# Attention steps at later, written-out places, a raised priority in the recurrent layer, and the low weight parts of the attention on GpSimd

## The chip, the cores and the metric

The kernel runs on one core of one Trainium2 chip. The time is device microseconds (us) of one execution, the median of three runs. The core has a matrix engine (TensorE, PE in the profile; its weight loads are the row PEld), VectorE (DVE), ScalarE (ACT), GpSimd (POOL) and SyncE (SP), which issues the transfers here.

## The reference

512 tokens of width 1024 pass through two layers in float32:

```python
# layer 0
h = h + hybrid_attention_mixer(rms_norm(h))   # 8 dilated heads ("A"), 4 differential heads ("B")
h = h + conv_ffn(rms_norm(h))                 # up 1024 -> 6144, causal conv3, gelu(g) * v, down
# layer 1
h = h + recurrent_mixer(rms_norm(h))          # gate branch * RG-LRU(conv4(x branch))
h = h + conv_ffn(rms_norm(h))
```

The mixer of layer 0 projects to q, k and v, normalises q and k per head, adds a bias that is linear in the distance, takes softmax rows and multiplies by v. A B head subtracts lambda times a second softmax from the first and normalises its output. In the recurrent mixer a block-diagonal product makes the gates r and i of each 128 channels, `a = exp(-8 r softplus(-a_param))`, `u = sqrt(1 - a^2) * (i * x)`, and a scan over time gives h.

## The kernel before

Activations are kept transposed, 128 channels by 512 tokens. Each float32 product is made of three float32r products: an operand is split into a high part (a cast on ACT) and a low part (the difference to it, rounded), and high x high, high x low and low x high are added in PSUM. So each weight tile that comes in is split: `split` (line 97) casts `wh` on ACT (line 100) and subtracts `wl` on DVE (line 102). Weights of the attention's projection come in units of 768 columns, all others in units of 1024. Four buffers each hold the raw, high and low units, and a unit is split two units before TensorE uses it (`AHEAD`).

**The attention.** Eight pairs of heads, first the four B heads (n = 0 to 3), then the eight A heads in pairs (n = 4 to 7), are each projected in a tile: four units by four blocks of 128 tokens, that is 16 steps of six matmuls of 384 columns (`group`, lines 339 to 341, tile `pj`). The 128 steps stand in a list, `line`; behind them come 28 steps of three matmuls of 512 columns, the part of the output projection that needs only finished heads (`early_out`). All other work on TensorE in the attention is placed behind one of these steps by hand, with `place(step, f)`, and TensorE's order is kept as written (`pe`). Step 16 n + 15 ends the projection of tile n; then follow:

- `qk_norm` at once, urgent, on ACT and DVE; `qk_transpose` 8 steps later (`qkt`, line 389).
- The attention proper, whose offsets count from step 16 n + 26. Three batches of scores (`sc`, line 419, tiles `S`), for the query blocks (0, 1), (2) and (3), each followed by its softmax: DVE adds the bias and takes the maximum (line 430), ACT takes the exponential (433); in an A pair ACT scales the row (490), in a B head DVE subtracts the second softmax from the first (535).
- The transposes of the four blocks of probabilities (`tr`, line 440, tile `pt`), each copied out by ACT (`pth`, 443) and DVE (`ptl`, 444); an A pair has two per block.
- The product with v (`out`, lines 453 to 463, tile `O`), two of them in an A pair, and the copies out of PSUM (505 to 510 in A; 546, 548 in B).
- In a B head the norm: a sum over channels on TensorE (`obms`, line 553), two steps on ACT and five on DVE (558 to 562), then the split (564, 565).

The offsets come from `spread`, which lays the pieces and some empty places evenly over 15.5 steps. Scores, transposes, outputs and norms share four PSUM banks. On ACT and DVE the order is a scheduler's: among what is ready it takes what comes first in the program, or has been given high priority, and the order is then fixed.

**The recurrent layer.** For each of eight blocks of channels, `lru_in` multiplies by the input weights, runs the convolution (677, 679, 681) and splits the result (`xrh`, 792; `xrl`, 794); `lru_gates` makes two products of three matmuls (`pr`, `pi`) in two PSUM banks, whose readers are sigmoids on ACT (809, 810). Between the gates of n = 3 and the input of n = 5, `lru_scan` takes the first four blocks through exponential, square, root (820, 822, 828) and the scan on DVE (830). Sigmoids, exponentials and roots are kept in program order on ACT by `after`, as each switch loads a table.

Of the kernel before, what the change touches and what calls it, by code (L numbers as in the profile page):

```python
# [12 lines left out]
F32 = mybir.dt.float32  # L13
F32R = mybir.dt.float32r
AF = mybir.ActivationFunctionType
ALU = mybir.AluOpType
# [7 lines left out]
NB = S // P  # L24
# [6 lines left out]

QK_LAG = 8
AT_LAG = 11
SPAN = 15.5

BATCHES = ((0, 1), (2,), (3,))
GAP = 3
TAIL_A = 3
TAIL_B = 3
TOK = 1  # L40
EARLY = 4
V_BUFS = 3
# [21 lines left out]
def trunk(  # L64
# [16 lines left out]
    V, A, T, G = nc.vector, nc.scalar, nc.tensor, nc.gpsimd  # L81
# [7 lines left out]
    mm = ctx.enter_context(tc.tile_pool(name="mm", bufs=4, space=PSUM))  # L89

    uid = [0]

    def nm(s):
        uid[0] += 1
        return f"{s}{uid[0]}"

    def split(src, n=1024):

        hi = whp.tile([P, n], F32R, tag="wh", name=nm("wh"))
        A.copy(hi, src)  # L100
        lo = wlp.tile([P, n], F32R, tag="wl", name=nm("wl"))
        V.tensor_tensor(lo, src, hi.bitcast(F32), ALU.subtract)  # L102
        return hi, lo

    def load(ap, n=1024, parts=1):
# [6 lines left out]
    def wunit(ap, n=1024):  # L112
        return split(load(ap, n), n)
# [10 lines left out]
    def prefetch(n):  # L124
        while todo and len(ready) < n:
            ready.append(wunit(*todo.pop(0)))

    def next_unit():

        prefetch(AHEAD + 1)  # L130
        return ready.pop(0)
# [71 lines left out]
    with ExitStack() as actx:  # L203
# [113 lines left out]
        def group(n, u, b):  # L317

            t = tiles[n]
            if b == 0:  # L320
                if u == 0:
                    t["banks"] = [mm.tile([P, S], F32, tag="mm", name=nm("pj")) for _ in range(NB)]
                if n == 0:
                    if u == 0:
                        t["units"] = first_tile()
                    t["w"] = t["units"][u]
                    prefetch(min(u, 2))
                else:
                    t["w"] = next_unit()
            if n == 0 and u == 3 and b == TOK:  # L330
                with tc.high_priority():
                    token_stats(x_acc[0])
            wh, wl = t["w"]
            tb = slice(b * P, (b + 1) * P)
            o = t["banks"][b][:, :CW]
            for j in range(2):
                k = 2 * u + j
                cw = slice(j * CW, (j + 1) * CW)
                pe(T.matmul(o, xs[k][0][:, tb], wh[:, cw], start=k == 0, stop=False))  # L339
                pe(T.matmul(o, xs[k][1][:, tb], wh[:, cw], start=False, stop=False))  # L340
                pe(T.matmul(o, xs[k][0][:, tb], wl[:, cw], start=False, stop=k == KC - 1))  # L341
            if u == 3 and (n or b >= TOK):
                with tc.high_priority():
                    for e in range(b + 1) if n == 0 and b == TOK else (b,):
                        evacuate(n, e)
# [126 lines left out]
            oT[p] = (hi, lo)  # L472
            return hi, lo

        def nothing():
            pass

        def attn_a(n):

            p = ORDER[n]  # L480
            st = {}

            def sc(blocks):
                if blocks[0] == 0:
                    st["b"] = [head_bias(2 * p + s) for s in range(2)]
                rows = products(tiles[n]["qk"], blocks)
                for i in blocks:
                    for s in range(2):
                        e, r = softmax_row(rows[s, i], i, st["b"][s])
                        A.activation(e, e, AF.Copy, scale=r)  # L490
                        st["e", s, i] = e

            def tr(s, i):
                if i == 0:
                    st["pt", s] = pt_tiles()
                transposed(st["e", s, i], i, *st["pt", s])

            def out(s):
                ps = bank("O")
                pv(ps, tiles[n]["v"], *st["pt", s], s)  # L500
                if s == 0:
                    st["o"] = smp.tile([P, S], F32, tag="o", name=nm("o"), bufs=1)
                    st["t"] = smp.tile([P, S], F32, tag="t", name=nm("t"), bufs=1)
                lo_half, own = ((ps[HD:], slice(0, HD)), (ps[:HD], slice(HD, P)))[s]
                A.copy(st["t"][own], lo_half)
                V.tensor_tensor(st["o"][own], ps[own], st["t"][own], ALU.add)
                if s == 1:
                    hi, lo = o_tiles(p)
                    A.copy(hi, st["o"])
                    V.tensor_tensor(lo, st["o"], hi.bitcast(F32), ALU.subtract)  # L510

            return spread(
                [partial(sc, b) for b in BATCHES],
                [[partial(tr, s, i) for s in range(2)] for i in range(NB)],
                [partial(out, 0), partial(out, 1)], TAIL_A)

        def attn_b(n):

            p = ORDER[n]
            st = {}  # L520

            def sc(blocks):
                if blocks[0] == 0:
                    st["b"] = head_bias(4 + p)
                rows = products(tiles[n]["qk"], blocks)
                for i in blocks:
                    for c in range(2):
                        st[i, c] = softmax_row(rows[c, i], i, st["b"])
                        if c == 0:
                            e0, r0 = st[i, 0]  # L530
                            A.activation(e0, e0, AF.Copy, scale=r0)
                        else:
                            (e0, _), (e1, r1) = st[i, 0], st[i, 1]
                            V.tensor_tensor(r1, r1, lam, ALU.mult)
                            V.scalar_tensor_tensor(e0, e1, r1, e0, ALU.mult, ALU.add)

            def tr(i):
                if i == 0:
                    st["pt"] = pt_tiles()
                transposed(st[i, 0][0], i, *st["pt"])  # L540

            def out():
                o_ps = bank("O")
                pv(o_ps, tiles[n]["v"], *st["pt"])
                st["o"] = smp.tile([P, S], F32, tag="sq", name=nm("ob"))
                A.copy(st["o"], o_ps)
                st["sq"] = smp.tile([P, S], F32, tag="sm3", name=nm("obsq"))
                A.activation(st["sq"], o_ps, AF.Square)

            def norm():  # L550
                o = st["o"]
                ps = bank("obms")
                pe(T.matmul(ps, ones, st["sq"], start=True, stop=True))
                y = smp.tile([P, S], F32, tag="sm3", name=nm("oby"))
                A.activation(y, ps, AF.Ln, bias=epsb)
                A.activation(y, y, AF.Exp, scale=-0.5)
                t = smp.tile([P, S], F32, tag="sq", name=nm("obt"))
                V.tensor_tensor(t, y, y, ALU.mult)
                V.scalar_tensor_tensor(t, ps, EPS, t, ALU.add, ALU.mult)
                V.tensor_scalar(t, t, -0.5 * (1.0 - LAM_INIT), 1.5 * (1.0 - LAM_INIT), ALU.mult, ALU.add)  # L560
                V.tensor_tensor(y, y, t, ALU.mult)
                V.scalar_tensor_tensor(o, o, col(C_BS), y, ALU.mult, ALU.mult)
                hi, lo = o_tiles(p)
                A.copy(hi, o)
                V.tensor_tensor(lo, o, hi.bitcast(F32), ALU.subtract)

            return spread(
                [partial(sc, b) for b in BATCHES], [[partial(tr, i)] for i in range(NB)],
                [out] + [nothing] * TAIL_B + [norm], TAIL_B)

        def spread(scs, trs, outs, tail):

            gap = [nothing] * GAP
            s = [scs[0]] + gap + [scs[1]] + gap + [scs[2]]
            for i, tr in enumerate(trs):
                s += tr + [nothing] * (GAP if i + 1 < NB else tail)
            return s + outs


        early = []  # L580
# [24 lines left out]
        def place(g, f):  # L605
            at.setdefault(int(g), []).append(f)
# [12 lines left out]
        for n in range(NT):  # L619
            place(16 * n + 15, partial(urgent, qk_norm, n))  # L620
            place(16 * n + 15 + QK_LAG, partial(qk_transpose, n))
            steps = (attn_a if ORDER[n] < 4 else attn_b)(n)
            for k, f in enumerate(steps):
                place(16 * n + 15 + AT_LAG + k * SPAN / len(steps), f)
        for g in range(max(len(line), max(at) + 1)):
            if g < len(line):
                line[g]()
# [212 lines left out]

    prev = None
    for n in range(KC):
        cur = lru_in(n)
        if prev is not None:
            lru_gates(n - 1, *prev)
        if n == KC // 2:
            lru_scan(range(KC // 2))
        prev = cur
# [92 lines left out]
```

## Time and profile before

| | |
|---|---|
| median of 3 runs | 1210.08 us (1209.28 to 1210.39) |
| the profiled execution | 1209.16 us, span of its instructions 1207.4 us |
| mean granted TensorE clock | 0.997 of full speed |
| TensorE busy | 1186.1 us (98%), 5566 matmuls |
| DVE, ACT busy | 810.3 us (67%), 581.9 us (48%) |
| GpSimd busy | 0.7 us |

The attention lasts until about 245 us of the span, the recurrent layer's gates lie between 680 and 735 us, and the rest are projections and feed-forward layers. A matmul's end is modelled in the profile, so a wait is shown a little shorter than the distance between two starts. The granted clock is the share of full speed (2.4 GHz) that the chip allowed TensorE; 0.5 is its lower level.

### The profile page before, as it was taken

To read this page: it belongs to the slowest core of one execution; us is meant where nothing else is said; L and a number is where in the kernel's file an instruction comes from. 1 tells how busy PE (TensorE), PEld (TensorE's weight loads), DVE (VectorE), ACT (ScalarE), POOL (GpSimd) and SP (SyncE) were. 2 spreads that over 40 slices of the span, in tenths; PEclk is the share of its full clock that TensorE was granted. 3 is DMA by queue.
4 is the path that set the end of the run, shared out by engine and by line. 5 is a ranking of instruction groups with operands and counts; after the bars stand their busy time and mean duration, and the time that the engine had idled before them with its cause. 6 is when DMAs were issued, how large, how long until landed. Compare 5 with 4: busy or idle time off the path is not lost.

```text
span 1207.4 us, 14660 instructions
## 1 busy us (share of the span) xinstructions
PE 1186.1 (98%) x5566; PEld 989.9 (82%) x5566; DVE 810.3 (67%) x1333; ACT 581.9 (48%) x972; POOL 0.7 (0%) x6
## 2 busy tenths in 40 slices
PE   8999999999999999999999999999999999999998
PEld 8988888778888888888888778888888888888887
DVE  7878877677777773577446887767777763577431
ACT  7666787655444441344224688545444432344220
POOL 0000000000000000000000000000000000000000
PEclk9999999999999999999999999999999999999999
DMA  7221122053323233232323312433233332323221
GB/s 252 79 67 53 53 70 80 19 174 105 105 88 105 89 103 96 97 103 90 104 88 105 117 41 74 136 93 100 91 102 95 98 100 93 105 88 105 88 87 53
DMA packets 33766, 114.31 MB, mean 95 GB/s; under 512 B 3872, under 2 KB 4384, under 8 KB 33696
## 3 DMA queue, kind: packets, MB, share of 16 engines
q1 hardware_dynamic: 33552, 113.37, 29.6%
q8 instruction: 44, 0.72, 0.2%
q14 instruction: 26, 0.21, 0.1%
q10 hardware_dynamic: 144, 0.00, 0.0%
HBM read 111.27 MB, written 2.10 MB: 94 GB/s over the span
## 4 chain that ended last, share of the span: by engine, by line
PE 87%; ACT 7%; DVE 5%; DMA 1%; issue 1%; SPq 0%; ACTq 0%; DVEq 0%
PE mm L116 26%; PE mm L118 26%; PE mm L117 26%; ACT sm L433 2%; PE pj L339 1%; PE pj L341 1%; PE pj L340 1%; PE pt L440 1%; ACT sm L490 1%; DMA raw<-in_w_att_dram 1%; PE qkt L389 1%; ACT wh L100 1%; ACT qkraw L359 1%; DVE wl L102 1%; ACT v L362 0%
## 5 line engine op out<-in xcount | busy, mean ns | idle before, releaser
L116 PE MATMUL mm<-xh,wh 128*128 128x512 f32 x896 | 350.2, 391 | 0.0
L117 PE MATMUL mm<-xl,wh 128*128 128x512 f32 x896 | 349.1, 390 | 0.0
L118 PE MATMUL mm<-xh,wl 128*128 128x512 f32 x896 | 349.0, 390 | 0.0
L100 ACT CAST wh<-raw 128x1024 fp32r<-128x1024 f32 (+1 forms) x207 | 211.4, 1024 | 274.8 <-PE mm L117 245.0
L102 DVE TENSOR_TENSOR wl<-raw,wh 128x1024 fp32r<-128x1024 f32 (+1 forms) x207 | 244.8, 1183 | 42.9 <-ACT wh L100 39.6
L117 PEld LDWEIGHTS mm<-xl,wh 128*128 128x128 f32 x896 | 168.4, 188 | 35.7 <-issue 0.7
L116 PEld LDWEIGHTS mm<-xh,wh 128*128 128x128 f32 x896 | 168.4, 188 | 35.6 <-issue 0.7
L118 PEld LDWEIGHTS mm<-xh,wl 128*128 128x128 f32 x896 | 168.3, 188 | 35.2
L681 DVE SCALAR_TENSOR_TENSOR cv<-us,pt,cv 128x511 f32<-128x511 f32 (+2 forms) x216 | 160.9, 747 | 4.8 <-ACT cv L679 1.2
L116 PE MATMUL mm<-fh,wh 128*128 128x512 f32 x384 | 149.4, 389 | 0.0
L117 PE MATMUL mm<-fl,wh 128*128 128x512 f32 x384 | 149.4, 389 | 0.0
L118 PE MATMUL mm<-fh,wl 128*128 128x512 f32 x384 | 149.4, 389 | 0.0
L677 DVE TENSOR_TENSOR us<-mm,rs 128x512 f32<-128x512 f32 x104 | 71.5, 688 | 94.5 <-PE mm L118 94.4
L711 DVE TENSOR_TENSOR h<-mm,h 128x512 f32<-128x512 f32 x48 | 33.2, 691 | 141.5 <-PE mm L118 141.5
L339 PE MATMUL pj<-wh,xh 128*128 128x384 f32 x256 | 93.4, 365 | 1.6 <-ACT wh L309 0.5
L702 ACT CAST fh<-cv 128x512 fp32r<-128x512 f32 x48 | 29.8, 621 | 126.4 <-DVE cv L699 126.4
L679 ACT ACTIVATE cv<-us,pt 128x512 f32<-128x512 f32 x104 | 84.6, 813 | 11.4 <-DVE us L677 11.2
L341 PE MATMUL pj<-wl,xh 128*128 128x384 f32 x256 | 86.7, 339 | 1.0 <-DVE wl L102 1.0
L340 PE MATMUL pj<-wh,xl 128*128 128x384 f32 x256 | 86.1, 336 | 0.0
L116 PEld LDWEIGHTS mm<-fh,wh 128*128 128x128 f32 x384 | 72.1, 188 | 15.0
L118 PEld LDWEIGHTS mm<-fh,wl 128*128 128x128 f32 x384 | 72.1, 188 | 15.0
L117 PEld LDWEIGHTS mm<-fl,wh 128*128 128x128 f32 x384 | 72.1, 188 | 15.0
(190 smaller groups left out, 1233.3 us busy)
## 6 DMA issues: line engine op xcount, KB each, us to landing
raw<-in_w_up_dram SPq DMA_DIRECT2D x96, 512.0 KB, 3.5
raw<-in_w_dn_dram SPq DMA_DIRECT2D x48, 512.0 KB, 3.5
raw<-in_w_att_dram SPq DMA_DIRECT2D x31, 384.0 KB, 3.1
raw<-in_w_ri_dram SPq DMA_DIRECT2D x16, 512.0 KB, 3.5
raw<-in_w_ao_dram SPq DMA_DIRECT2D x8, 512.0 KB, 3.8
raw<-in_w_ro_dram SPq DMA_DIRECT2D x8, 512.0 KB, 3.5
raw<-in_xT_dram SPq DMA_DIRECT2D x7, 512.0 KB, 4.6
out_dram<-h SPq DMA_DIRECT2D x8, 256.0 KB, 2.0
```

Of the source, the lines that this page charges most:

```text
L100: A.copy(hi, src)
L102: V.tensor_tensor(lo, src, hi.bitcast(F32), ALU.subtract)
L116: order(T.matmul(out, wh, xh, start=first, stop=False))
L117: order(T.matmul(out, wh, xl, start=False, stop=False))
L118: return order(T.matmul(out, wl, xh, start=False, stop=last))
L339: pe(T.matmul(o, xs[k][0][:, tb], wh[:, cw], start=k == 0, stop=False))
L340: pe(T.matmul(o, xs[k][1][:, tb], wh[:, cw], start=False, stop=False))
L341: pe(T.matmul(o, xs[k][0][:, tb], wl[:, cw], start=False, stop=k == KC - 1))
L677: V.tensor_tensor(u, ps, state["rs"], ALU.mult)
L679: A.activation(c, u, AF.Identity, scale=col(wcol + (taps - 1) * stride), bias=col(bcol))
L681: V.scalar_tensor_tensor(c[:, d:], u[:, : S - d], col(wcol + (taps - 1 - d) * stride), c[:, d:], ALU.mult, ALU.add)
L711: V.tensor_tensor(h[m], ps, h[m], ALU.add)
```

## The change

- The offsets are written out. Scores stay at 0, 2, 4 in all tiles. Transposes of a B tile go from steps 4, 6, 8, 10 to 6, 8, 10, 13, its output product from 12 to 15, its norm from 14 to 17, which is behind the first scores of the next tile (16). An A pair's transposes go from 4 and 5, 7 and 7, 9 and 10, 12 and 12 to 6 and 7, 8 and 9, 10 and 11, 13 and 14, its two output products from 14 and 15 to 15 and 16. `qk_transpose` of the next tile stays at 13.
- `split` subtracts the low part on GpSimd instead of DVE for units of 768 columns, once the first step of the line is under way (`warmed`): the units of the first pair stay on DVE.
- `lru_in` and `lru_gates` of the recurrent layer, except the last gates, get high priority.

```diff
-SPAN = 15.5
...
-GAP = 3
-TAIL_A = 3
-TAIL_B = 3
+
+SC_AT = (0, 2, 4)
+TR_AT = (6.5, 8.7, 10.9, 13.1)
+OUT_AT = 15
+NORM_AT = 17
...
+    warmed = []
...
-        V.tensor_tensor(lo, src, hi.bitcast(F32), ALU.subtract)
+        (G if n == 768 and warmed else V).tensor_tensor(lo, src, hi.bitcast(F32), ALU.subtract)
...
                     t["w"] = t["units"][u]
+                    warmed.append(u)
                     prefetch(min(u, 2))
...
-            return spread(
-                [partial(sc, b) for b in BATCHES],
-                [[partial(tr, s, i) for s in range(2)] for i in range(NB)],
-                [partial(out, 0), partial(out, 1)], TAIL_A)
+            steps = [(g, partial(sc, b)) for g, b in zip(SC_AT, BATCHES)]
+            steps += [(g + s, partial(tr, s, i)) for i, g in enumerate(TR_AT) for s in range(2)]
+            return steps + [(OUT_AT + s, partial(out, s)) for s in range(2)]
...
-            return spread(
-                [partial(sc, b) for b in BATCHES], [[partial(tr, i)] for i in range(NB)],
-                [out] + [nothing] * TAIL_B + [norm], TAIL_B)
-
-        def spread(scs, trs, outs, tail):
-
-            gap = [nothing] * GAP
-            s = [scs[0]] + gap + [scs[1]] + gap + [scs[2]]
-            for i, tr in enumerate(trs):
-                s += tr + [nothing] * (GAP if i + 1 < NB else tail)
-            return s + outs
+            steps = [(g, partial(sc, b)) for g, b in zip(SC_AT, BATCHES)]
+            steps += [(g, partial(tr, i)) for i, g in enumerate(TR_AT)]
+            return steps + [(OUT_AT, out), (NORM_AT, norm)]
...
-            for k, f in enumerate(steps):
-                place(16 * n + 15 + AT_LAG + k * SPAN / len(steps), f)
+            for g, f in steps:
+                place(16 * n + 15 + AT_LAG + g, f)
...
-        cur = lru_in(n)
-        if prev is not None:
-            lru_gates(n - 1, *prev)
+        with tc.high_priority():
+            cur = lru_in(n)
+            if prev is not None:
+                lru_gates(n - 1, *prev)
```

## Rows read from the trace of the kernel before

**Rows 1.** The page, busy time of TensorE: us, share, instructions.

```profile
PE 1186.1 (98%) x5566; PEld 989.9 (82%) x5566; DVE 810.3 (67%) x1333; ACT 581.9 (48%) x972; POOL 0.7 (0%) x6
```

**Rows 2.** Waits of TensorE: us in total, times, longest.

```profile
PE pt L440 <- DVE sm L535: 5.2, 6, 1.4
PE pt L440 <- DVE ptl L444: 3.1, 2, 1.8
PE pt L440 <- DVE rst L168: 2.9, 1, 2.9
PE pr L116 <- ACT xrh L792: 2.0, 1, 2.0
...
PE mm L116 <- ACT oh L509: 0.6, 1, 0.6
```

**Rows 3.** Busy us of each engine, then granted clock, in windows of the attention.

```profile
core 0: us, PE busy (x) PEld busy (x) DVE busy (x) ACT busy (x) POOL busy (x), PEclk, DMA share, GB/s
...
90.00:120.00 30.00, 28.20 (x178) 24.96 (x177) 24.34 (x69) 18.59 (x52) 0.00 (x0) 1.00 0.20 59
...
180.00:210.00 30.00, 28.17 (x179) 25.29 (x179) 23.58 (x68) 23.25 (x66) 0.00 (x0) 1.00 0.27 88
```

**Rows 4.** Timeline of TensorE in a B tile: start, us, instruction, [idle before].

```profile
87.90 1.02 PE L553 MATMUL obms<-obsq,ones 128*128 128x512 f32 x2
...
102.45 0.34 PE L341 MATMUL pj<-wl,xh 128*128 128x384 f32 x1
104.21 0.55 PE L440 MATMUL pt<-ident,sm 128*128 128x128 f32 x3 [1.43 <-DVE sm L535]
104.52 0.42 PE L339 MATMUL pj<-wh,xh 128*128 128x384 f32 x1
...
106.53 0.34 PE L341 MATMUL pj<-wl,xh 128*128 128x384 f32 x1
```

**Rows 5.** Windows around the wait of n = 6, columns as in rows 3.

```profile
210.00:213.00 3.00, 1.19 (x6) 0.62 (x4) 2.27 (x7) 3.00 (x8) 0.00 (x0) 1.00 0.01 5
213.00:216.00 3.00, 1.92 (x8) 1.56 (x9) 2.55 (x10) 3.00 (x10) 0.00 (x0) 0.73 0.01 3
216.00:219.00 3.00, 3.00 (x15) 2.54 (x14) 2.65 (x5) 0.74 (x2) 0.00 (x0) 0.70 0.02 5
```

**Rows 6.** Timeline of TensorE in the recurrent layer.

```profile
716.29 0.39 PE L116 MATMUL mm<-xh,wh 128*128 128x512 f32 x1
716.52 0.39 PE L117 MATMUL mm<-xl,wh 128*128 128x512 f32 x1
718.93 0.50 PE L116 MATMUL pr<-xrh,gwh 128*128 128x512 f32 x1 [2.02 <-ACT xrh L792]
```

**Rows 7.** Windows behind that wait, columns as in rows 3.

```profile
719.00:721.00 2.00, 2.00 (x6) 1.62 (x7) 1.98 (x3) 1.54 (x2) 0.00 (x0) 0.64 0.17 14
721.00:723.00 2.00, 2.00 (x6) 1.51 (x6) 2.00 (x4) 0.00 (x0) 0.00 (x0) 0.50 0.66 246
```

**Rows 8.** Timeline of DVE in the B tile of rows 4.

```profile
91.07 0.69 DVE L559 SCALAR_TENSOR_TENSOR obt<-obms,obt 128x512 f32<-128x512 f32 x1
...
101.22 0.96 DVE L102 TENSOR_TENSOR wl<-raw,wh 128x768 fp32r<-128x768 f32 x1
...
103.55 0.61 DVE L535 SCALAR_TENSOR_TENSOR sm<-sm,sum,sm 128x384 f32<-128x384 f32 x1
```

**Rows 9.** Waits of all engines: ACT's for the norm of a B tile.

```profile
ACT oh L564 <- DVE ob L562: 13.8, 4, 3.5
```

**Rows 10.** Groups of DVE by line and form: busy us, mean ns.

```profile
L102 DVE TENSOR_TENSOR wl<-raw,wh 128x768 fp32r<-128x768 f32 x31 | 29.6, 953 | 13.2 <-ACT wh L100 13.0
```

**Rows 11.** Groups of GpSimd, columns as in rows 10.

```profile
masks.py:199 POOL TENSOR_SCALAR_AFFINE_SELECT ident<-ident 128x128 f32<-128x128 f32 x1 | 0.3, 294 | 0.1
```

**Rows 12.** Timeline of ACT in the recurrent layer.

```profile
710.31 0.80 ACT L679 ACTIVATE cv<-us,pt 128x512 f32<-128x512 f32 x1
...
713.01 0.68 ACT L810 ACTIVATE u<-pi,pt 128x512 f32<-128x512 f32 x1
...
718.25 0.62 ACT L792 CAST xrh<-cv 128x512 fp32r<-128x512 f32 x1 [2.07 <-DVE cv L681]
```

More of the change, by code (lines that the diff above doesn't have):

```diff
@@ L473, in o_tiles @@
             return hi, lo
-        def nothing():
-            pass
         def attn_a(n):
```

## The prediction

> **What bounds the kernel now.** I read the page's first part, the waits of TensorE, windows of 30 us, and then timelines around each wait. TensorE is busy for 1186.1 of 1207.4 us [rows 1]; the change can only be worth what TensorE loses, and I looked for where that is. Its waits stand in one short list, and the feed-forward layers are not in it. What matters of it [rows 2]: transposes of the probabilities (`pt`, line 440) wait 5.2 us in 6 places for DVE's `sm` at line 535 (the B tiles), 3.1 us in 2 places for `ptl` and 2.9 us in one place at line 168 (the A tiles); one gate product of the recurrent layer (`pr`) waits 2.0 us, and the output projection 0.6 us. In windows of the attention TensorE runs for about 28 of 30 us, DVE for 24, ACT for 19 to 23 [rows 3]: no engine is full, so it is the order that makes TensorE wait.
>
> What a wait really costs is more than the idle time printed, since ends of matmuls are modelled. In a B tile TensorE's instructions follow each other every 0.18 us (11 steps from 104.52 to 106.53), and the wait at 104.21 follows its predecessor by 1.76 us: 1.6 us lost for 1.43 printed [rows 4]. With 0.16 us added at each of nine places, the `pt` waits cost 6.1 us (B), 3.4 us (tiles n = 4 and 5) and 3.1 us (n = 6), together 12.6. After the last one the granted clock is 0.73 and 0.70 in two stretches of 3 us [rows 5], that is, TensorE at its lower level (1.2 GHz) for some 3.4 us, which costs 1.7 us more; it had idled 2.89 us. After the 1.8 us of n = 5 [rows 2] the window has the full clock, 1.00 [rows 3]. The gate product is alike: 718.93 - 716.52 - 0.23 = 2.2 us lost [rows 6], then 0.64 and 0.50 of the clock over 4 us [rows 7], 1.7 us more: 3.9 us in all. Everything that can be won is so 12.6 + 1.7 + 3.9 + 0.6 = 18.8 us.
>
> **Part by part. Transposes later in B tiles.** A step of the line (six matmuls) lasts 6 x 0.18 = 1.1 us. A B tile's transposes move from offsets 4, 6, 8, 10 to 6, 8, 10, 13, so the two that wait get 2.2 and 3.3 us of other projection matmuls as cover, against 1.6 and 0.6 us lost. At the same time TensorE loses less, so ACT and DVE must do a tile in some 2 us less. DVE can: before the waited `sm` it does a `wl` of 0.96 us at 101.22 [rows 8], which goes away. And the norm, whose five DVE operations ACT waits out for up to 3.5 us per B tile [rows 9], moves behind the next tile's first scores, whose softmax then starts without it. The 6.1 us go. Against that: the norm's sum of squares now holds one of four PSUM banks while three batches of scores want two each. It is held from 87.90 to the end of line 559 at 91.76, 3.9 us [rows 4, 8]; from offset 17 to the third batch at 20 there are three steps, 3.3 us. That is between 0 (another bank is free) and 0.6 us for each of four tiles behind a B tile; I take half, 1.2 us. Net gain 4.9, bounds 3.7 and 6.1.
>
> **Transposes later in A tiles.** Here most of the third block's transposes move by one step (9 to 10, 10 to 11). What they wait for is a PSUM bank, held until the first transposes are copied out, and that copy stands on ACT behind all the exponentials: ACT is busy for all of 210 to 213 us while TensorE has 1.19 of 3 us [rows 5]. ACT keeps all its work, so the offload to GpSimd does not shorten this; one step does: 1.1 us each for n = 4 and 5, 2.2 of 3.4 us. For n = 6 the line has already turned to output products of three matmuls, 3 x 0.23 = 0.7 us a step [rows 6], so 0.7 of 3.1 us goes; the 2.2 us left (2.89 - 0.7) are still above the 2.02 after which the clock fell, so I leave the 1.7 us in. Lower bound nothing, upper bound all (8.2 us with the clock).
>
> **The end of the attention.** The last tile's second output product moves from step 153 to 154 of 155. One step less lies over the chain of copy, add, round that the first output projection waits for (0.6 us now): 0.7 us more.
>
> **Low parts on GpSimd.** Of the 31 `wl` instructions of 768 columns, 28 leave DVE (three stay with the first pair), 28 x 0.953 = 26.7 us [rows 10]. The trace has no two-input arithmetic on GpSimd. Its nearest row is a 128x128 select of 0.294 us [rows 11], six times the width gives 1.8 us as an upper estimate; the lower bound is DVE's 0.95. The latency doesn't show: units are split two ahead, eight steps of 1.1 us before TensorE needs them, and GpSimd has only four such operations per tile, 7 us of 25. Nothing else is queued on GpSimd behind them. The raw buffers come free up to 0.9 us later; there are four, and no wait of TensorE in the attention's steady part comes from a transfer [rows 2]. So on TensorE's path this part costs 0; its gain is inside the B figure. If that cover were gone, each late unit would cost TensorE 1.8 - 0.95 us, 24 us in all.
>
> What could speak against it is that the two engines disturb each other. The trace of before cannot show it, as GpSimd does nothing beside DVE in it but set-up [rows 11]. The Trainium skill, in "SBUF — State Buffer", Who interferes with whom, says that a DVE instruction with two SBUF inputs and a GpSimd instruction that reads SBUF exclude each other for their whole length, whichever starts second waiting. No run yet shows it; by that rule `sm` at line 535 and the norm's products can be held up, and the price is that of the last rival below. The Trainium skill, "GPSIMD Engine Reference", 3.1 Elementwise, gives 4497 ns of a two-input add for 2048 columns, so an estimate of 1.7 us for 768; the sum would be the same.
>
> **Priority in the recurrent layer.** `xrh` of n = 5 comes at 718.25 because its convolution's ACT step (line 679) stands behind the whole first scan, at 710.31, and the rest of the chain takes 8 us more among the scan's DVE steps [rows 12]. Raised ahead of the scan, both go earlier. But the same product also needs the two PSUM banks that the gates of n = 4 free, and these stay behind the scan by an explicit order: the second is read until 713.01 + 0.68 = 713.7 [rows 12]. Work put ahead of the scan (the step of 0.80 us, the rounding of 0.62 us, a weight cast or so) moves that to some 716. That is 3 us before the product ran (718.93), and next to where TensorE came to it (716.52) [rows 6]. So the wait goes if the order on TensorE stays about as it is: 3.9 us. Bounds: all 3.9, or, if the product is put a job earlier (some 29 matmuls of 0.23 us before 716.5, around 710), a wait of 5.8 us plus the clock's 1.7, which is 3.6 us worse than now.
>
> **The sum.** 4.9 + 2.2 + 0.7 - 0.7 + 3.9 = 11.0 us. The profiled execution took 1209.16 us with a span of 1207.4; 1209.2 - 11.0 = 1198.2. The median of the runs is 0.9 above the profiled one, so 1199.
>
> **Rivals.**
> *The A waits go too.* ACT begins the softmax of n = 4 only behind the norm's rounding [rows 9], and between A tiles behind the output chain; if it now begins earlier, the 1.2 + 2.4 + 1.7 us left also go: 1199.1 - 5.3 = 1193.8. Against it: ACT is full in that stretch [rows 5].
> *The gate product waits for its banks instead of for its input.* Place as above, the price between no gain (1203) and 3.6 us worse (1206.6). For it: the banks come free by my reckoning within half a microsecond of when TensorE arrives.
> *New waits in the attention eat its gain* (banks for the scores, the output product behind later transposes): about 7 us lost again, 1206.
> *Slower: GpSimd holds DVE up.* If each of its four operations per tile stopped DVE for its whole 1.8 us, DVE would lose 7.0 and gain 3.8 us, 3.2 more per tile on six tiles, 19.2 us: 1199.1 + 19.2 = 1218. It turns the result from 11.0 / 6 = 1.8 us a tile on. Against it: the operands of most DVE steps on that path (scores, transposes, projections) lie in PSUM, and there is now room. The rule of the Trainium skill named above is this rival.
> That the offload does not happen can be left out: the condition is met for every unit of 768 columns after the first step.
>
> **How the numbers follow.** Chances: forecast 0.47, A waits too 0.18, gate banks 0.18, new waits 0.10, GpSimd slows DVE 0.05, other 0.02. A measurement here tells 0.2% (2.4 us) from no change. Forecast and first rival are faster for sure, the gate rival nearly so; new waits may come out within 0.2%; with the last, slower: faster 0.85, same 0.08, slower 0.07. The range goes from everything gone but the tail (1192.5) to the gate banks at their worst (1207).
>
> **What would show it.** B tiles: no wait of `pt` for line 535, each tile some 2 us shorter. A tiles: waits of some 0.5 to 1 us left at line 440, one above 2 us near n = 6 with a clock below 1. Recurrent layer: no `pr` wait, clock 1.00. GpSimd: 28 operations of 1 to 2 us and about 27 us less on DVE. Wrong would be a wait of `S` for banks, `pr` waiting for line 810, or line 535 lasting longer than its 0.61 us for 384 columns.

## The result, and the profile after

The change makes the kernel slower: 1256.0 us (median of 4 runs, 1253.5 to 1259.3) against 1209.7 on the same chip, a ratio of 1.038 with a 95% interval of 1.036 to 1.041. The forecast was 1199. The profiled execution has a span of 1252.5 us, 45.1 more than before, in two places: the last wait of the attention (`mm` for `oh`) stands at 262.73 us instead of 245.96, 16.8 later, and the other 28.3 us are lost in the recurrent layer.

The page after, busy time, answers to [rows 1]: TensorE idles for 31.5 us more and is busy 13.6 us longer with the same 5566 matmuls (part of them at the lower clock), and DVE is no less busy than before although 28 instructions have left it.

```profile
PE 1199.7 (96%) x5566; PEld 999.1 (80%) x5566; DVE 814.8 (65%) x1305; ACT 582.8 (47%) x972; POOL 54.9 (4%) x34
```

The waits of TensorE after (us in total, times, longest) answer to [rows 2]. Line numbers have moved: `pt` 440 is 444, `pr` 116 is 119, `sm` 535 is still 535, `wh` 100 is 103.

```profile
PE mm L119 <- ACT wh L103: 13.1, 2, 12.1
PE qkt L393 <- DVE qkraw L384: 11.4, 7, 3.9
PE mm L119 <- DVE us L669: 7.3, 1, 7.3
PE pj L343 <- DVE v L367: 5.1, 4, 1.6
PE pt L444 <- DVE ptl L448: 2.8, 2, 2.1
PE S L423 <- DVE ql L398: 2.7, 2, 2.4
PE mm L121 <- DVE wl L105: 1.7, 1, 1.7
```

What the forecast wanted gone is gone: no `pt` waits for line 535, none for 168, and no `pr` waits for `xrh` (two of 0.9 and 0.2 us for others are left). In their place stand waits for other DVE instructions of the attention (`qkraw`, `v`, `ql`) and three of the recurrent layer that were not there at all. No wait of TensorE names GpSimd: its low parts are never late.

What is late is seen in the groups (busy us, mean ns), first the new one on GpSimd, then some of DVE up to 262 us of the span.

```profile
L105 POOL TENSOR_TENSOR wl<-raw,wh 128x768 fp32r<-128x768 f32 x28 | 54.2, 1938 | 154.5 <-ACT wh L103 120.1 <-DVE bias L408 19.9 <-PE pj L345 14.5
```

```profile
L384 DVE TENSOR_TENSOR qkraw<-qkraw,rsy 128x512 f32<-128x512 f32 x16 | 16.8, 1093 | 0.2
L534 DVE TENSOR_TENSOR sum<-sum,lam 128x1 f32<-128x1 f32 x16 | 7.4, 465 | 0.3
L171 DVE TENSOR_TENSOR rst<-rst,ms 128x16 f32<-128x16 f32 x8 | 4.5, 560 | 0.1
L408 DVE TENSOR_SCALAR bias<-dist_b 128x512 f32<-128x512 f32 x4 | 3.1, 786 | 0.0
```

The same groups before:

```profile
L380 DVE TENSOR_TENSOR qkraw<-qkraw,rsy 128x512 f32<-128x512 f32 x16 | 10.3, 683 | 0.1
L534 DVE TENSOR_TENSOR sum<-sum,lam 128x1 f32<-128x1 f32 x16 | 2.5, 155 | 0.2
L168 DVE TENSOR_TENSOR rst<-rst,ms 128x16 f32<-128x16 f32 x8 | 1.3, 168 | 0.1
L404 DVE TENSOR_SCALAR bias<-dist_b 128x512 f32<-128x512 f32 x4 | 1.7, 419 | 0.0
```

A mean hides how this happens; the timeline after of one B tile shows it, first GpSimd, then DVE:

```profile
76.22 1.84 POOL L105 TENSOR_TENSOR wl<-raw,wh 128x768 fp32r<-128x768 f32 x1 [10.30 <-ACT wh L103]
79.95 2.29 POOL L105 TENSOR_TENSOR wl<-raw,wh 128x768 fp32r<-128x768 f32 x1 [1.90 <-ACT wh L103]
86.08 1.84 POOL L105 TENSOR_TENSOR wl<-raw,wh 128x768 fp32r<-128x768 f32 x1 [3.83 <-ACT wh L103]
```

```profile
77.04 0.68 DVE L559 SCALAR_TENSOR_TENSOR obt<-obms,obt 128x512 f32<-128x512 f32 x1
...
80.46 1.80 DVE L534 TENSOR_TENSOR sum<-sum,lam 128x1 f32<-128x1 f32 x1
...
86.33 1.88 DVE L408 TENSOR_SCALAR bias<-dist_b 128x512 f32<-128x512 f32 x1
```

The product of one column per partition at 80.46, 0.16 us of work, ends at 82.26, just when GpSimd's instruction does (82.24); everything behind it in DVE's order is 1.6 us late. The bias at 86.33 is held as well: 1.88 us instead of 0.42, until 0.29 us behind the end of GpSimd's instruction (87.92). GpSimd's instruction from 79.95 is itself 0.45 us longer than the other two; when it started, `ob` of line 562, with its inputs in SBUF, was under way (79.79 to 80.53). Line 559 at 77.04, one of whose inputs lies in PSUM (`obms`), runs beside GpSimd in 0.68 us, as it did before without it (0.69, [rows 8]). The clock pays too: over the first two stretches of 100 us the granted clock is 0.98 and 0.95, before it was 1.00 in both.

In the recurrent layer the timeline after, TensorE, ACT and DVE together, shows both large waits:

```profile
702.75 3.89 ACT L103 CAST wh<-raw 128x1024 fp32r<-128x1024 f32 x4 [4.25 <-PE mm L120]
...
704.14 1.02 PE L652 MATMUL nrm<-acc,ones 128*128 128x512 f32 x2
...
706.54 0.68 ACT L654 ACTIVATE rs<-nrm,epsb 128x512 f32<-128x512 f32 x1
...
711.61 1.89 DVE L669 TENSOR_TENSOR us<-mm,rs 128x512 f32<-128x512 f32 x3
...
712.45 0.77 PE L119 MATMUL mm<-xh,wh 128*128 128x512 f32 x1 [7.29 <-DVE us L669]
...
773.27 1.28 ACT L812 ACT_TABLE_LOAD   x1
...
782.98 2.93 ACT L103 CAST wh<-raw 128x1024 fp32r<-128x1024 f32 x3
784.06 0.80 PE L119 MATMUL mm<-xh,wh 128*128 128x512 f32 x1 [12.13 <-ACT wh L103]
```

Before, TensorE had the norm and the first gate product here:

```profile
669.13 1.02 PE L660 MATMUL nrm<-acc,ones 128*128 128x512 f32 x2
...
681.04 0.50 PE L116 MATMUL pr<-xrh,gwh 128*128 128x512 f32 x1
```

After, the norm `nrm` is computed only behind the projections of four blocks, 96 matmuls, where before it stood behind the first block's 24; the four casts raised with them stand ahead of the norm's first step on ACT, so `us`, which frees the projections' banks, comes at 711.61. Later all projections have been used up ahead of the gates, and nothing is left to run under the second scan (ACT from 773.27): TensorE waits until the scan's last root is through and the first cast behind it is made. Before, 48 matmuls of projections ran between `nrm` and the first gate product, while ACT and DVE made the norm. The granted clock pays here as well (window 760 to 780 us 0.87, 780 to 800 us 0.61).

### The profile page after: what moved, and what is told of

Same layout as the page of the kernel before. It is cut to its first block, busy times and chain, and to the rows that moved or that the text cites. A ratio compares the mean times of both kernels' runs of the same rounds, so it can differ in the third digit from the quotient of the medians.

```text
span 1252.5 us, 14696 instructions
## 1 busy us (share of the span) xinstructions
PE 1199.7 (96%) x5566; PEld 999.1 (80%) x5566; DVE 814.8 (65%) x1305; ACT 582.8 (47%) x972; POOL 54.9 (4%) x34
## 4 chain that ended last, share of the span: by engine, by line
PE 83%; DVE 9%; ACT 5%; issue 2%; DMA 1%; SPq 0%; DVEq 0%; ACTq 0%
PE mm L119 25%; PE mm L121 25%; PE mm L120 25%; PE pj L343 2%; PE pj L345 2%; PE pj L344 2%; DVE qkraw L384 1%; PE S L423 1%; ACT sm L437 1%; PE pt L444 1%; DVE u L822 1%; ACT wh L103 1%; PE qkt L393 1%; DMA raw<-in_xT_dram 1%; DVE wl L105 1%
## 5 line engine op out<-in xcount | busy, mean ns | idle before, releaser
L121 PE MATMUL mm<-xh,wl 128*128 128x512 f32 x896 | 344.5, 392 | 1.9 <-DVE wl L105 1.7
L120 PE MATMUL mm<-xl,wh 128*128 128x512 f32 x896 | 345.0, 392 | 0.0
L105 DVE TENSOR_TENSOR wl<-raw,wh 128x1024 fp32r<-128x1024 f32 (+1 forms) x179 | 218.1, 1222 | 31.7 <-ACT wh L103 28.7
L343 PE MATMUL pj<-wh,xh 128*128 128x384 f32 x256 | 96.1, 376 | 5.7 <-DVE v L367 5.1
```

What stands on the lines that cost most here:

```text
L105: (G if n == 768 and warmed else V).tensor_tensor(lo, src, hi.bitcast(F32), ALU.subtract)
L120: order(T.matmul(out, wh, xl, start=False, stop=False))
L121: return order(T.matmul(out, wl, xh, start=False, stop=last))
```

## The experiments

**The parts alone.** Three kernels each make one part of the change, a fourth all but the priority. The places alone are the change's hunks on `SPAN`, `spread`, `attn_a` and `attn_b`; the others:

```diff
 # GpSimd alone (and the lines of `warmed`)
 ...
-        V.tensor_tensor(lo, src, hi.bitcast(F32), ALU.subtract)
+        (G if n == 768 and warmed else V).tensor_tensor(lo, src, hi.bitcast(F32), ALU.subtract)
 ...
 # priority alone
 ...
+        with tc.high_priority():
             cur = lru_in(n)
             if prev is not None:
                 lru_gates(n - 1, *prev)
```

> The kernel before with the later places alone; all low parts on DVE, no priority in the recurrent layer. Theory 1 (the attention's 16.8 us of loss come from GpSimd shutting DVE out, and the later places are good): the pt waits of 11.2 us go at least by half, time 1200 to 1205 us. Theory 2 (the later places are the loss, through new waits of the key transposes and the score banks): attention about 17 us longer, time 1222 to 1228 us.

> The kernel before with the 28 low parts on GpSimd alone, at the old places. Theory 1: GpSimd holds DVE up by 1.1 us per operation (31 us in all, as in the changed kernel) and the old places have less cover, time 1225 to 1240 us. Theory 2: DVE gets 26.7 us of room and the pt waits shrink, time 1203 to 1210 us.

> The kernel before with the high priority of the recurrent layer's input and gates alone. Theory 1 (the priority pulls the projections ahead of the norm and the gates, so that nothing is left to cover the second scan): 28 us more, time 1234 to 1242 us, with waits of about 7 us before the convolution of the first block and 12 us before a gate projection. Rival (the loss needs the attention's change too, or comes from its clock): time 1205 to 1212 us.

> The changed kernel without the priority of the recurrent layer. If the two stages add up: before plus 16.8 us, 1225 to 1229 us, on either theory of the attention; the recurrent layer again has its single 2.0 us wait. If the stages do not add up, outside of 1222 to 1232 us.

| kernel | us | ratio to before (95%) | difference |
|---|---|---|---|
| before, same chip | 1210.2 | | |
| places alone | 1206.5 | 0.9970 (0.9959 to 0.9981) | -3.7 |
| GpSimd alone | 1235.0 | 1.0210 (1.0193 to 1.0227) | +24.8 |
| priority alone | 1237.0 | 1.0222 (1.0207 to 1.0238) | +26.8 |
| places and GpSimd | 1229.3 | 1.0169 (1.0141 to 1.0198) | +19.1 |

The parts add up: -3.7 + 24.8 + 26.8 = 47.9 against 46.4 for the whole change. The places gain, and each of the other two loses far more.

The waits of the places alone show the gain and what ate half of it:

```profile
PE qkt L393 <- DVE qkraw L384: 4.9, 4, 1.5
PE pt L444 <- DVE ptl L448: 2.1, 1, 2.1
PE pr L119 <- ACT xrh L784: 2.0, 1, 2.0
PE mm L119 <- ACT oh L510: 1.3, 1, 1.3
```

One of the four waits for `qkraw`, in the timeline of TensorE:

```profile
110.24 1.23 PE L393 MATMUL qkt<-ident,qkraw 128*128 128x128 f32 x8 [1.47 <-DVE qkraw L384]
```

With GpSimd alone the stretched groups are others than in the whole change, above all the one that the forecast had named as the sign (0.61 us before, [rows 8], and still 0.61 in the whole change, where no stop met it); TensorE waits for what follows it, now at the output product:

```profile
L537 DVE SCALAR_TENSOR_TENSOR sm<-sm,sum,sm 128x384 f32<-128x384 f32 x4 | 7.2, 1801 | 0.0
L171 DVE TENSOR_TENSOR rsy<-rsy,rst 128x16 f32<-128x16 f32 x8 | 6.0, 749 | 0.2
```

```profile
PE O L457 <- DVE ptl L446: 12.0, 4, 3.3
```

The page of this kernel shows that the 24.8 us are not waiting alone:

```profile
PE 1196.6 (97%) x5566; PEld 998.0 (81%) x5566; DVE 814.9 (66%) x1305; ACT 582.3 (47%) x972; POOL 53.6 (4%) x34
```

Of its span of 1231.3 us (23.9 more than before) TensorE idles for 34.7, which is 13.4 more, and it is busy 10.5 us longer with the same matmuls: the granted clock is 0.95 in both of the first two stretches of 100 us (1.00 before).

**Is it GpSimd's reading?** In three kernels DVE keeps every low part, and GpSimd does something that nobody waits for, at the same places in the program.

```diff
+        if n == 768 and warmed:
+            d = dmp.tile([P, 256], F32, ...)
+            for c in (slice(0, 256), slice(256, 512), slice(512, 768)):
+                G.tensor_tensor(d, src[:, c], hi[:, c].bitcast(F32), ALU.subtract)   # reads two
+                G.tensor_copy(d, hi[:, c].bitcast(F32))        # or: reads one
+            G.tensor_copy(d[:, :1], hi[:, :1].bitcast(F32))    # or: one column, and
+            for _ in range(6):
+                G.memset(d, 0.0)                               # writes only
```

> The kernel before, in which DVE still makes all low parts; GpSimd additionally makes the same 28 differences (three of 256 columns each, some 1.9 us per unit) into an unused scratch buffer. Nothing on another engine needs what GpSimd writes. Theory (GpSimd's reading of SBUF stops DVE's instructions with two SBUF inputs): the same DVE forms are stretched as in the run with the low parts on GpSimd (the difference over 384 columns from 0.61 us to over 1.2, the 128x16 products from 0.17 to over 0.4), and the time is at least as bad as that run's, 25 to 50 us above before, as DVE has kept its 26.7 us. Rival (the harm is that the low parts come later, from a slower engine): nothing is late here, so within 3 us of before and no form on DVE stretched.

> As the run in which GpSimd repeats the differences, but GpSimd only writes: one column copied from the high part (so that it starts at the same place), then six memsets of 256 columns into the scratch buffer. DVE keeps its work. Theory (two inputs from SBUF on GpSimd are what excludes DVE): DVE's forms keep their durations within 10% and the time stays within 4 us of before. Rival (any work of GpSimd, or its writes and semaphores, disturbs DVE): forms stretched in proportion to GpSimd's busy time, 10 us or more above before.

> As the run in which GpSimd repeats the differences into a scratch buffer, but each of the 84 is a copy of 256 columns of the high part: one input from SBUF instead of two. Nothing waits for them. Theory A (any read of SBUF by GpSimd excludes DVE's two-input forms): the same DVE forms are stretched, in proportion to GpSimd's busy time; with some 0.5 us a copy about half the loss of that run, 6 to 14 us above before. Theory B (only two-input instructions of GpSimd exclude DVE): the forms keep their durations within 10%, within 4 us of before.

| GpSimd beside an unchanged DVE | GpSimd busy us | us (before) | ratio (95%) | DVE busy us (810.3 before) |
|---|---|---|---|---|
| 84 differences, two inputs | 86.1 | 1226.6 (1208.5) | 1.0148 (1.0132 to 1.0163) | 830.4 |
| 84 copies, one input | 56.9 | 1212.5 (1210.1) | 1.0024 (1.0012 to 1.0036) | 815.7 |
| memsets, almost only writes | 70.6 | 1210.0 (1208.5) | 1.0012 (1.0003 to 1.0021) | 810.9 |

Groups of DVE with the differences, then with the copies, then with the memsets: two products with both inputs in SBUF, and a scaling with one.

```profile
L173 DVE TENSOR_TENSOR rst<-rsy 128x16 f32<-128x16 f32 x8 | 4.0, 500 | 0.7 <-ACT rsy L171 0.7
L174 DVE TENSOR_TENSOR rst<-rst,ms 128x16 f32<-128x16 f32 x8 | 3.2, 398 | 0.1
L380 DVE TENSOR_SCALAR ms<-ms 128x16 f32<-128x16 f32 x8 | 2.9, 368 | 0.1
```

```profile
L173 DVE TENSOR_TENSOR rst<-rsy 128x16 f32<-128x16 f32 x8 | 2.3, 293 | 0.7 <-ACT rsy L171 0.7
L174 DVE TENSOR_TENSOR rst<-rst,ms 128x16 f32<-128x16 f32 x8 | 1.9, 241 | 0.1
```

```profile
L174 DVE TENSOR_TENSOR rst<-rsy 128x16 f32<-128x16 f32 x8 | 1.4, 170 | 0.7 <-ACT rsy L172 0.7
L175 DVE TENSOR_TENSOR rst<-rst,ms 128x16 f32<-128x16 f32 x8 | 1.4, 170 | 0.1
...
L381 DVE TENSOR_SCALAR ms<-ms 128x16 f32<-128x16 f32 x8 | 2.1, 257 | 0.1
```

The first run settles that it is no lateness: nothing needs what GpSimd makes, and 18 us are lost. GpSimd's reading does hold the raw buffers, and 26 transfers wait for it, by 2.9 us at most; but between 25 and 245 us no cast waits for a transfer and no matmul for a weight part, so that is not the loss. The 18 us are less than the 25 to 50 expected; in three short pieces each stop is shorter, and the 384-column difference happened to meet none of them (608 ns), so that part of the expectation failed. Writes leave the two-input products alone (0.17 us, as before). Copies fall between the theories: the same products are stretched, but by at most some 0.2 us each, and 2.4 us are lost, not 6 to 14.

**Which raised instructions hurt?**

```diff
 # chain raised                             # jobs raised
         ps = job(xs)                       +        with tc.high_priority():
+        with tc.high_priority():           +            ps = job(xs)
+            xr = conv(...); xh, xl = ...           xr = conv(...); xh, xl = ...
 ...
+            with tc.high_priority():
+                lru_gates(n - 1, *prev)            lru_gates(n - 1, *prev)
```

> The kernel before, in which only the convolution, its split and the gates of the recurrent layer get high priority, and the projections (job) keep theirs. Theory (the loss of the recurrent change comes from projections pulled ahead of the norm and of the scan's cover): the order of the projections stays, the 7.3 us wait for us and the 12.1 us wait for wh don't appear, the 2.0 us wait of the first gate product goes with its clock loss of 1.7 us: 1206 to 1208, that is 2 to 4 us faster. Rival (raising the chain delays the scans or casts themselves): the wait for wh behind the second scan stays and the time is 10 us or more above before.

> The kernel before, in which only the projections (job) of the recurrent layer's input get high priority, not the convolution and the gates. Theory (pulled projections are the loss): both new waits are there again, 7 us for us and some 12 us for wh behind the second scan, 20 to 27 us above before. Rival (the raised chain is the loss): within 4 us of before.

The chain alone: 1207.4 against 1208.5, ratio 0.9988 (0.9979 to 0.9997), and 2.6 us less in the span of the profiled executions. The wait of the first gate product shrinks from 2.0 to two of 0.6 and 0.2, and the window from 720 to 740 us has the full clock (0.93 before). The projections alone: 1228.5, ratio 1.0168 (1.0155 to 1.0182), +20.0, with these waits new:

```profile
PE mm L116 <- DVE us L677: 8.6, 2, 7.3
...
PE mm L116 <- ACT wh L100: 4.6, 2, 3.6
```

So the projections are the cause of 20.0 of the 26.8 us. The expected 12 us behind the second scan did not come. The wait of 3.6 us for a cast stands behind the first scan, and through the second (ACT from 763.40) TensorE has no wait:

```profile
750.79 0.80 PE L116 MATMUL mm<-xh,wh 128*128 128x512 f32 x1 [3.60 <-ACT wh L100]
```

Only with the chain raised as well does the cast of the gate input's weights fall behind the whole second scan, with its wait of 12.1 us. With both raised 6.8 us more are lost than with the projections alone; that this cast is the reason is read from the traces, no run shows it apart. The chain alone does no harm.

**What the runs point to.** The places and the raised chain, with nothing on GpSimd; then `QK_LAG` 9 instead of 8, which puts `qk_transpose` one step later, at 14 in the tile; then `AT_LAG` 12 on top.

```diff
-QK_LAG = 8
-AT_LAG = 11
+QK_LAG = 9        # second and third
+AT_LAG = 12       # third
```

> The later places, and high priority for the recurrent chain (convolution, split, gates) without the projections; nothing on GpSimd. Theory (the two act in different layers and add): 3.7 from the places and 1.2 to 2.6 from the chain, so 4.9 to 6.3 us below before; the 4.9 us waits of qkt for qkraw stay. Rival (they share a cause): not below the run with the places alone, 3.7.

> As the run with later places and raised chain, with qk_transpose one step (1.1 us) later, at 14 instead of 13 in its tile. Theory (the scaling of qkraw ends when it did in the kernel before, and TensorE comes to qkt too early because the output product no longer stands ahead of it): of four waits of 1.2 to 1.5 us at most 0.4 us each stay, so 3 to 4.5 us faster than that run, 8 to 10 below before. Rival (DVE takes the slack, qkraw simply comes later, or the scores now wait for ql): the waits stay in sum, within 1.5 us of that run.

> As the run before in this list, with the whole attention of each tile one step later as well (scores at 27 instead of 26), so that the scores keep their distance from qk_transpose. Theory (the one step of qk_transpose was enough and S does not wait): 0.5 to 1.5 us slower than it, as the last tile ends a step later and the output projection waits for oh that much longer (1.3 to some 2.4 us). Rival (S waited for ql in it): that wait goes, and this is the faster by 1 us or more.

Against 1208.7 before on the same chip: 1203.2, ratio 0.9959 (0.9945 to 0.9974); 1199.3, ratio 0.9924 (0.9911 to 0.9937); 1211.5, ratio 1.0026 (1.0017 to 1.0035). The first lies 5.5 us below before, so the two parts add. The second, 9.4 below, is the best kernel of the study. Its waits:

```profile
PE pt L444 <- DVE ptl L448: 2.1, 1, 2.1
...
PE qkt L393 <- DVE qkraw L384: 0.7, 2, 0.3
```

One step of 1.1 us took 4.1 of the 4.8 us of `qkt` waits away. The third kernel is 12 us slower than the second, which neither theory expected: `pt` waits for line 535 again, and `qkt` for `qkraw`.

```profile
PE pt L444 <- DVE sm L535: 3.8, 3, 1.4
PE qkt L393 <- DVE qkraw L384: 3.0, 3, 1.0
```

Against the first of the three, all places have kept their distances to each other and moved against the projection, with which `qk_norm` and the weight splits go. Which of DVE's instructions then comes first is the scheduler's choice; why this choice costs so much was not settled.

## Why the prediction was wrong, step by step

- **B tiles' transposes: right.** The six waits for line 535, 6.1 us with what the idle times leave out, are gone in every run with the later places (but the last kernel), and the norm in its bank makes no score wait: the 1.2 us set aside for it were 0. **What was missing** is the neighbour. The text of the change said that `qk_transpose` stays at 13 while the output product goes from 12 to 15; that product had been the cover of `qk_transpose`, as `qkraw` is scaled just before (DVE at 109.29 us before, 109.41 with the places alone). Before, the product ran from 109.83 to 111.84 us and `qkt` came at 112.78, without a wait; with the places alone the work before it ends at 108.77 and it starts at 110.24. So TensorE comes to `qkt` too early in four tiles: 4.9 us printed, some 5.5 lost. In the forecast this stood only as the pooled rival of new waits, and for banks. The kernel with `QK_LAG` 9 confirms it.
- **A tiles and the end: right within a microsecond.** n = 4 and 5 lose 0.9 us instead of 3.4 (forecast 1.2), n = 6 waits 2.1 instead of 2.9, the output projection 1.3 instead of 0.6.
- So the places came to -3.7 instead of -4.9 - 2.2 - 0.7 + 0.7 = -7.1.
- **"So on TensorE's path this part costs 0": the first step that failed.** The premise was checked for lateness, and lateness indeed costs nothing. But GpSimd stops DVE, and the part costs 24.8 us alone and 22.8 on top of the places. The rival that said so had a chance of 0.05, on the ground that most of DVE's operands on the path lie in PSUM. That looked at the large instructions. The stop falls on a small one with two SBUF inputs, or with one and a scalar (128x1, 128x16), as hard as on a large one, and everything behind it in order waits. DVE lost 26.7 us of low parts and yet was 4.5 us busier, so 31.2 / 28 = 1.1 us of stretch for each of GpSimd's instructions. The rival's price, 19.2 us, came near by luck, for its sum was not right either: it counted six tiles, though 28 instructions are four in each of seven, and it set DVE's saving against the stops; with the measured 1.1 us that is four stops a tile less 3.8, which is 0.7 and below its own turning point of 1.8. What DVE's saving was worth was not measured apart; whatever it was, 24.8 us are lost on top of it. The stops fall in the chain that TensorE waits for (13.4 us more idle time with GpSimd alone), and the lower clock, which neither the forecast nor this rival had priced for this part, makes its busy time 10.5 us longer.
- The Trainium skill, "SBUF — State Buffer", Who interferes with whom, sides with every one of these readings: a DVE instruction with two SBUF inputs is excluded by a GpSimd instruction that reads SBUF, not by one that only writes (0.50 us with differences, 0.17 with memsets); scalings can be excluded by both (0.37 and 0.26 us against 0.17); an instruction with an input in PSUM by neither (line 559, 0.68 us beside GpSimd). What the runs do not bear out is a stop of the full length: a copy takes 0.67 us in the profile and stops DVE for 0.2 at most, a difference of 256 columns 1.02 us and 0.54.
- **"The wait goes if the order on TensorE stays about as it is": the second step that failed,** by the condition it named. The order did not stay: `lru_in` contains `job`, and a raised `job` moves 24 matmuls with their weight casts per block. The worst bound, 3.6 us, looked at one gate product moved by one job. It should have asked what the raised work is moved past: the norm, which frees the banks of that same work, and the stretches in which it covered the scans. The term was -3.9, the runs give +26.8, of which raised projections alone +20.0. What was raised on purpose in the forecast's reasoning, the chain, gives -1.2 (interval -0.4 to -2.5).

## What to carry to other kernels

Before work goes to an idle GpSimd, count not how busy the engines are but which DVE instructions with two SBUF inputs (or one and a scalar) run at that time in the chain that TensorE waits for; each can be held for most of the length of a two-input instruction of GpSimd (1.65 of 1.84 us here), however small it is itself. A raised priority moves everything inside its braces, weight casts too: raise the short chain that is late and leave the long independent work where it covers something. When a piece of the matrix engine's work is moved past another, ask what it had been covering.

## What the runs showed that was not expected

- GpSimd's difference of 128x768 takes 1.94 us in the mean, with stops of DVE up to 1.65 us (128x1: 0.155 to 1.80 us); pieces of 256 columns stop it for up to 0.54 us (128x16: 0.17 to 0.71). Per column both are 2.1 ns.
- After the same wait of 2.1 us near n = 6 the clock differed between two profiled executions. With the places alone, then with the raised chain too (windows, columns as in rows 3):

```profile
210.00:240.00 30.00, 28.34 (x156) 22.45 (x157) 18.18 (x53) 20.08 (x53) 0.00 (x0) 0.94 0.07 19
```

```profile
210.00:240.00 30.00, 28.97 (x167) 22.64 (x167) 18.67 (x55) 20.03 (x52) 0.00 (x0) 1.00 0.05 19
```

The mean clock of the seven runs with the places alone goes from 0.996 to 1.000, so the execution may decide and not the kernel. The 1.7 us that the forecast left in for it are thus not certain at this length of wait; what decides was not tried.
